# Attention in two passes over the halves of the frames, with the output projection's jobs by halves

## The chip, the cores and the metric

The kernel runs on one core of a Trainium2 chip. Time is device microseconds (us), from the start of one execution to its end; several executions are timed and their median is taken. Besides, one execution is profiled, and all rows of the profile are from that one. TensorE (PE) multiplies, VectorE (DVE), ScalarE (ACT) and GpSimd (POOL) work on tiles, and SyncE (SP) issues nearly all DMA transfers, in the order of the program. Each engine carries out its own instructions in order.

## What is computed

One block of a streaming encoder over 16 meta tokens and 1024 frames (L = 1040), model width 1024, in fp32: 8 attention heads of 64 with a forget gate and causal mask, beside a pooling branch; both go through one output projection; then a SwiGLU with its own RMS norm.

```python
def _layer(h, norm1_w, w_in, b_fgate, ...):
    proj = _rmsnorm(h, norm1_w) @ w_in
    q, k, v, fg, u = jnp.split(proj, ...)
    q, k = _rmsnorm(q, q_norm_w), _rmsnorm(k, k_norm_w)      # per head
    cum_logf = jnp.cumsum(log_sigmoid(fg + b_fgate), axis=-1)
    a_out = _forgetting_attention(q, k, v, cum_logf)
    # s = q.k / 8 + cum_logf[t] - cum_logf[s], s <= t; softmax; @ v
    p_out = pooled(u) @ w_pool * pool_scale
    h = h + jnp.concatenate([a_out, p_out], -1) @ w_out
    n2 = _rmsnorm(h, norm2_w)
    return h + (silu(n2 @ w_gate) * (n2 @ w_up)) @ w_down
```

## The kernel before

A product of fp32 operands is made of three matmuls: each operand is split into a high part (ACT rounds it) and a low part (POOL or DVE subtracts), and high x high, low x high and high x low are summed in PSUM. Tiles are 128 partitions by up to 512 columns; the frames are held in two halves of 512 columns, `b` = 0 and 1.

The stages follow each other: input projections and the pooling branch (to some 247 us), attention (to some 478 us), gate and up, and the down projection. Between attention and gate/up lies the second norm, made for each half by itself.

**Attention's units.** The list `units` (L757) sets the order of pairs (head h, half b): head by head with both halves, and for the last two heads both first halves, then both second halves. A unit with b = 0 has three steps, one with b = 1 has seven; a step is one to three tiles of 128 key rows. In a step, `front` makes the scores `st` on PE (L672 to L675) and two exps on ACT, the rounded `ph` (L682) and the full `p` (L683); `mid`, one step later, subtracts them into `pl` (L689) on POOL, each fourth on DVE (`SUBV`); `back`, three steps later (`LA`), multiplies with v into `pv` (L702 to L704). After a unit's last step come Ln and Exp of the sum on ACT (L713, L714) and three passes on DVE (L720 to L723) that divide. With every second head, a background piece splits the result into `mh` and `ml` (L731, L732).

Ahead of a unit its row maxima must be known. `mx_steps` makes scores `s` on PE (L620 to L623) and reduces them on DVE (L624); `mt` collects them into `Mc` (L636 to L638), PE transposes it (L643), and ACT writes it into the operand Q (L644). The table `MAXN` says how many of these pieces run in each step of each unit, for the unit after it.

**Operands.** `stack(h)` (L573 to L586) loads Q1, Q2, K1 and K2 of a head for both halves, six large transfers over 64 partitions each and two small ones; `vload(h)` loads v. The split operands lie in DRAM from the projections on.

**Jobs that fill PE.** The output projection is cut into jobs that `fill` takes from the queue `fill_q`, as many a step as the table `FILL` says. `out_job` (L543) makes a half of one of eight row tiles: first 16 half-jobs for the pooling branch (12 matmuls `o`, L496 to L498), then 16 for head pairs 0 and 1 (6 matmuls). DVE adds each to h (L555). The w_out operand of a job is loaded two jobs ahead and split one job ahead (L525 ACT, L526 POOL). Head pairs 2 and 3 have jobs of their own, `c_job` (L831), with operands `wc` that `wc_prep` splits once (L826, L827); they also square the result (L836, ACT) and sum the squares for the second norm (L840). The eight `c_job`s of half 0 and then `first_half` stand at the queue's end.

**The passage.** `first_half` (L922) sends half 0 to DRAM, and puts pieces into the work queue `pq`: the second norm (`norm2`: split, two matmuls with ones `n` L859 and L860, then L861, Ln and Exp L865 and L866, three passes L146 to L148), the eight normalised tiles (`x_half` L875, `x_split` L880 and L881, tile `cb`), and between them `w0_prep`, the splits of gate/up's first weights. `work` takes `XW` pieces a step in the last unit. After attention `first_pair(0, second_half)` runs gate and up's first two products on half 0 (matmuls `gu`, L1277 to L1279), 12 for each of eight tiles `cb`, and between them `second_half` runs the `c_job`s of half 1 (table `CJ`), after which the norm of half 1 follows.

Of the kernel before, what the change touches and what calls it, by code (L numbers as in the profile page):

```python
# [48 lines left out]
def block_kernel(ctx, tc, hT, n1w, w_f, w_v, w_u, w_qk, b_f, qnw, knw, w_pool, pscale, w_out, n2w, w_g, w_up, w_d, outT):  # L49
# [453 lines left out]
    jobs = []

    def out_load(x):
        mix_of, ks, m, first = jobs[x]
        n = 128 * sum(k1 - k0 for k0, k1 in ks)
        s, o = (hs if n <= 512 else aux)(n, FT, "wos"), 0
        for k0, k1 in ks:
            nc.sync.dma_start(s[:, o:o + 128 * (k1 - k0)], w_out[m, :, k0:k1, :].rearrange("p k f -> p (k f)"))  # L510
            o += 128 * (k1 - k0)
        return s

    def h_load(x):
        if x < len(jobs) and jobs[x][3] and h2[jobs[x][2]] is None:
            h2[jobs[x][2]] = ut(SEQ, FT, "h2")
            nc.sync.dma_start(h2[jobs[x][2]], hT[:, jobs[x][2], META:])
# [952 lines left out]
```

## Time and profile before

| | us |
|---|---|
| median of 3 runs | 1154.95 (1151.79 to 1155.16) |
| the profiled execution | 1152.21 |
| its span, first to last instruction | 1150.4 |
| PE busy in the span | 1120.1 (97%) |
| DVE, ACT, POOL busy | 779.7, 482.9, 217.2 |

The profiled execution's rows add up to its own time, 1152.21 us, and not to the median. PE's busy time is modelled from the starts of matmuls, so two rows of a timeline overlap; what a matmul costs in a stream is the distance of the starts. An idle time in brackets is that of the engine right before the row, with what ended it. The granted clock is given in parts of full speed; the two levels are 1.2 and 2.4 GHz.

### The profile page before, as it was taken

How to read it: one execution, taken by the hardware profiler on the slowest of the kernel's cores; microseconds unless marked ns; L12 is line 12 of the kernel's file. 1: busy time of each engine (PE TensorE's matmuls, PEld its weight loads, DVE VectorE, ACT ScalarE, POOL GpSimd, SP SyncE). 2: the span in 40 equal slices, each digit the busy share in tenths (PEclk: the TensorE clock that was granted, in tenths of full speed). 3: DMA queues.
4: the chain of work that ended last, by engine and by line, in shares of the span. 5: the costliest groups of instructions: out<-in, count | busy, mean ns of one | idle time of the engine just before them, and what ended most of it. 6: DMA issues, size and time to landing. Idle time of an engine off the chain costs nothing.

```text
span 1150.4 us, 14630 instructions
## 1 busy us (share of the span) xinstructions
PE 1120.1 (97%) x5327; PEld 929.0 (81%) x5327; DVE 779.7 (68%) x1292; ACT 482.9 (42%) x871; POOL 217.2 (19%) x185
## 2 busy tenths in 40 slices
PE   7999999999999999698999999999999999999998
PEld 6778899778888888486788888888888888888886
DVE  7555873774557665858876656666666679778986
ACT  7344531635556456535433232323232335344541
POOL 0011245133445366100012111211121010000000
PEclk9999999999999999899999999999999999999999
DMA  7134341664543722140213122313131389643452
GB/s 241 71 129 153 113 147 45 185 203 102 145 95 84 160 69 81 67 146 19 101 57 109 63 94 63 110 56 101 65 110 55 126 285 349 199 149 101 156 192 110
DMA packets 62424, 141.09 MB, mean 123 GB/s; under 512 B 7616, under 2 KB 18496, under 8 KB 62352
## 3 DMA queue, kind: packets, MB, share of 16 engines
q1 hardware_dynamic: 52528, 123.86, 34.1%
q10 hardware_dynamic: 9824, 16.30, 3.9%
q8 instruction: 42, 0.69, 0.2%
q14 instruction: 30, 0.25, 0.1%
HBM read 105.17 MB, written 34.77 MB: 122 GB/s over the span
## 4 chain that ended last, share of the span: by engine, by line
PE 89%; DVE 8%; ACT 2%; issue 1%; DMA 0%; ACTq 0%; SPq 0%; DVEq 0%
PE gu L1119 11%; PE gu L1120 11%; PE gu L1118 11%; PE d L1379 6%; PE d L1377 6%; PE d L1378 6%; PE pj L448 3%; PE pj L449 3%; PE pj L447 3%; PE o L496 3%; PE o L498 3%; PE o L497 3%; PE st L675 2%; DVE cb L881 2%; PE v L255 2%; PE v L257 2%
## 5 line engine op out<-in xcount | busy, mean ns | idle before, releaser
L1118 PE MATMUL gu<-cb,ws 128*128 128x512 f32 x560 | 220.5, 394 | 1.1 <-ACT ws L1108 1.1
L1119 PE MATMUL gu<-cb,ws 128*128 128x512 f32 x560 | 220.6, 394 | 0.2 <-DVE ws L1109 0.2
L1120 PE MATMUL gu<-cb,ws 128*128 128x512 f32 x560 | 220.4, 393 | 0.0
L1108 ACT ACTIVATE ws<-wst 128x512 fp32r<-128x512 f32 x120 | 70.1, 623 | 143.3 <-DVE wst L1103 97.1
L1118 PEld LDWEIGHTS gu<-cb,ws 128*128 128x128 f32 x560 | 105.2, 188 | 26.0 <-ACT ws L1108 1.5
L1119 PEld LDWEIGHTS gu<-cb,ws 128*128 128x128 f32 x560 | 105.2, 188 | 25.0 <-DVE ws L1109 0.5
L1120 PEld LDWEIGHTS gu<-cb,ws 128*128 128x128 f32 x560 | 105.2, 188 | 24.4
L1109 DVE TENSOR_TENSOR ws<-wst,ws 128x512 fp32r<-128x512 f32 x120 | 82.4, 688 | 59.6 <-ACT ws L1108 59.6
L1377 PE MATMUL d<-hd,wd 128*128 128x512 f32 x308 | 121.0, 393 | 0.0
L1379 PE MATMUL d<-hd,wd 128*128 128x512 f32 x308 | 121.0, 393 | 0.0
L1378 PE MATMUL d<-hd,wd 128*128 128x512 f32 x308 | 120.9, 392 | 0.0
L1132 POOL TENSOR_TENSOR e<-e,e 128x512 f32<-128x512 f32 x20 | 29.1, 1456 | 371.6 <-DVE e L1145 199.9
L689 POOL TENSOR_TENSOR pl<-p,ph 128x512 fp32r<-128x512 f32 (+4 forms) x66 | 72.7, 1113 | 57.7 <-ACT p L683 51.5
L448 PE MATMUL pj<-xh,wl 128*128 128x346 f32 (+2 forms) x216 | 72.8, 337 | 0.0
L449 PE MATMUL pj<-xl,wh 128*128 128x346 f32 (+2 forms) x216 | 72.8, 337 | 0.0
L447 PE MATMUL pj<-xh,wh 128*128 128x346 f32 (+2 forms) x216 | 72.8, 337 | 0.0
L624 DVE TENSOR_REDUCE mp<-s 128x1 f32<-128x264 f32 (+8 forms) x112 | 52.5, 504 | 27.8 <-PE s L623 25.6
L682 ACT ACTIVATE ph<-st 128x512 fp32r<-128x512 f32 (+4 forms) x88 | 46.2, 525 | 53.9 <-PE st L675 48.9
L1378 PEld LDWEIGHTS d<-hd,wd 128*128 128x128 f32 x308 | 57.9, 188 | 13.3
L1379 PEld LDWEIGHTS d<-hd,wd 128*128 128x128 f32 x308 | 57.8, 188 | 13.3
L1377 PEld LDWEIGHTS d<-hd,wd 128*128 128x128 f32 x308 | 57.8, 188 | 13.2
L1048 ACT ACTIVATE hd<-wst 128x512 fp32r<-128x512 f32 x77 | 48.0, 623 | 36.3 <-issue 27.1
(288 smaller groups left out, 2385.4 us busy)
## 6 DMA issues: line engine op xcount, KB each, us to landing
wst<-in_w_d SPq DMA_DIRECT2D x77, 256.0 KB, 6.1
wst<-in_w_g SPq DMA_DIRECT2D x22, 512.0 KB
wst<-in_w_up SPq DMA_DIRECT2D x22, 512.0 KB, 3.4
wst<-hidd SPq DMA_DIRECT2D x22, 512.0 KB, 3.4
K<-kd SPq DMA_DIRECT2D x24, 260.0 KB, 7.5
vsd<-vst SPq DMA_DIRECT2D x16, 384.0 KB, 2.3
Q<-qd SPq DMA_DIRECT2D x24, 256.0 KB, 6.0
wst<-in_w_d SPq DMA_DIRECT2D x11, 512.0 KB, 3.6
```

The costliest lines, as they stand in the source:

```text
L447: mm(p[:, :n], wh[:, W], xh[k][:, o:o + n], start=k == 0, stop=False)
L448: mm(p[:, :n], wl[:, W], xh[k][:, o:o + n], start=False, stop=False)
L449: mm(p[:, :n], wh[:, W], xl[k][:, o:o + n], start=False, stop=k == KT - 1)
L689: sub.tensor_tensor(pl[:sz, o0:o1], p32[:sz, o0:o1], f(ph)[:sz, o0:o1], op=OP.subtract)
L1108: A.activation(t[:, :512], src, AF.Copy)
L1109: E.tensor_tensor(t[:, 512:], src, f(t)[:, :512], op=OP.subtract)
L1118: mm(p, w[:, W], c[:, :512], start=k == 0, stop=False)
L1119: mm(p, w[:, Wl], c[:, :512], start=False, stop=False)
L1120: mm(p, w[:, W], c[:, 512:], start=False, stop=k == 3)
L1377: mm(p, w[:, W], h[:, LO], start=i == 0, stop=False)
L1378: mm(p, w[:, Wl], h[:, LO], start=False, stop=False)
L1379: mm(p, w[:, W], h[:, HI], start=False, stop=i == NPR - 1)
```

## The change

- `units` becomes all heads' first halves, then all heads' second halves (`n` counts them, 0 to 15).
- `stack(h, b)` and `vload(h, b)` load the operands of one unit: 512 columns of Q, and of K and v what the half needs (640 or 1040 rows of K). K and Q are loaded three to four units ahead, v one unit ahead.
- Jobs are made for a half: 16 for the pooling branch, 8 for half 0 over all four head pairs (12 matmuls, with the norm's squares), 8 for half 1 over pairs 0 and 1, and 8 for half 1 over pairs 2 and 3, which run between gate/up's matmuls. These last ones too load and split their operand one by one; `wc_prep` is gone.
- `first_half` is inserted at place 24 of the queue of jobs. The weight splits `w0_prep` go to the work queue at the start of the last unit, ahead of whatever `first_half` brings. `XW` is 2, and from unit 12 on each step takes one piece.
- `MAXN`, `FILL` and the first call of `max_next` are set for the new order.

```diff
-MAXN = [(2, 0, 0), (0, 2, 2, 2, 2, 2, 2)] * 6 + [(2, 2, 2), (2, 2, 2), (0, 1, 1, 1, 1, 0, 0), (0,) * 7]
+MAXN = [(2, 2, 1)] * 7 + [(3, 3, 3)] + [(2, 2, 1, 1, 1, 1, 1)] * 8
 SUBV = 4
 MID = 1
 VST = 3
 AGE = 2
 RAMP = 1
-FILL = [11 / 37] * 8 + [.75] * 6 + [2] * 2
-CJ, XW = {1: (0, 1), 2: (2, 3), 3: (4, 5), 4: (6, 7)}, 3
+FILL = [8 / 24] * 8 + [12 / 35] * 5 + [4 / 14] * 2 + [2 / 7]
+CJ, XW, XN = {1: (0, 1), 2: (2, 3), 3: (4, 5), 4: (6, 7)}, 2, 12
...
-    def out_job(x, b, p=None):
-        mix_of, ks, m, first = jobs[x]
-        if b == 0:
-            if x not in wo:
-                wo[x] = out_split(out_load(x))
+    def out_job(x, b):
+        mix_of, k0, k1, m, halves, norm = jobs[x]
+        if b == halves[0]:
             for y in (x + 1, x + 2):
                 if y < len(jobs) and y not in wo:
                     wo[y] = out_load(y)
             h_load(x)
             h_load(x + 1)
-        p = out_mm(mix_of(), wo[x], b) if p is None else p
+        p = out_mm(mix_of(b), wo[x])
         S = slice(512 * b, 512 * b + 512)
-        post.append(lambda: V.tensor_tensor(h2[m][:, S], p, h2[m][:, S], op=OP.add))
-        if b == 1:
+
+        def add():
+            V.tensor_tensor(h2[m][:, S], p, h2[m][:, S], op=OP.add)
+            if norm:
+                sq = hs(512, FT, "sq2")
+                A.activation(sq, h2[m][:, S], AF.Square)
+                if m == 0:
+                    acc[b] = sq
+                else:
+                    (V if b else G).tensor_tensor(acc[b], acc[b], sq, op=OP.add)
+        post.append(add)
+        if b == halves[0] and x + 1 < len(jobs):
+            wo[x + 1] = out_split(wo[x + 1])
+        if b == halves[-1]:
             wo.pop(x)
-        elif x + 1 < len(jobs):
-            wo[x + 1] = out_split(wo[x + 1])
-
-    def out_fill(need, mix_of, ks, ms, first):
-        for m in ms:
+
+    def out_jobs(need, mix_of, k0, k1, halves, norm=False):
+        for m in range(KT):
             x = len(jobs)
-            jobs.append((mix_of, ks, m, first))
-            fill_q.extend([(need, lambda x=x: out_job(x, 0)), (need, lambda x=x: out_job(x, 1))])
-
-
-
-    vhb = []
+            jobs.append((mix_of, k0, k1, m, halves, norm))
+            if need is not None:
+                fill_q.extend((need, lambda x=x, b=b: out_job(x, b)) for b in halves)
...
-    def stack(h):
+    def stack(h, b):
+
 
         dma = nc.sync.dma_start
         T, B = slice(0, 64), slice(64, 128)
         R = (T, B)[h % 2]
-        Q1, Q2, K1, K2 = heads[h] = ut(SEQ, FR, "Q1"), ut(SEQ, FR, "Q2"), ut(L, FR, "K1"), ut(L, FR, "K2")
-        q, k = [[qkd[c][h // 2, a, R, :n] for a in range(2)] for c, n in (("q", SEQ), ("k", L))]
+        n = 640 + 400 * b
+        Q, K1, K2 = ut(1024, FR, "Q"), ut(n, FR, "K1"), ut(n, FR, "K2")
+        Q1, Q2 = Q[:, :512], Q[:, 512:]
+        heads[h, b] = Q1, Q2, K1, K2
+        q, k = [[qkd[c][h // 2, a, R, S] for a in range(2)] for c, S in (("q", slice(512 * b, 512 * b + 512)), ("k", slice(0, n)))]
         for t, P, src in ((Q1, T, q[0]), (K1, T, k[0]), (Q1, B, q[0]), (K1, B, k[1]), (Q2, T, q[1]), (K2, T, k[0])):
             dma(f(t)[P], src)
-        dma(f(Q2)[64:66], f(KAT[0])[4 * h + 2:4 * h + 4, :SEQ])
-        dma(f(K2)[64:68], f(KAT[0])[4 * h:4 * h + 4])
...
-    units = [(h, b) for h in range(NH - 2) for b in range(2)] + [(h, b) for b in range(2) for h in (NH - 2, NH - 1)]
-    out_fill(0, lambda: mixp, ((4, 8),), range(0, 8), True)
-    out_fill(4, lambda: mixa[0:2], ((0, 2),), range(0, 8), False)
+    units = [(h, b) for b in range(2) for h in range(NH)]
+    out_jobs(0, mix_pool, 4, 8, (0, 1))
+    out_jobs(4, mix_heads(0, 4), 0, 4, (0,), True)
+    out_jobs(6, mix_heads(0, 2), 0, 2, (1,))
+    out_jobs(None, mix_heads(2, 4), 2, 4, (1,), True)
+    C1 = len(jobs) - KT
...
-    for m in range(KT):
-        fill_q.append((7, lambda m=m: c_job(m, 0)))
-
     def first_half():
         spill(range(KT), 0)
         norm_pieces(0, NB[0])
-        xp, wp = x_pieces(0), [[(None, lambda u=u, n=n: w0_prep(u, n)) for n in ns for u in range(2)] for ns in ((11, 21), (12, 22))]
-        pq.extend(xp[:5] + wp[0] + xp[5:] + wp[1])
-
-    fill_q.append((7, first_half))
+        pq.extend(x_pieces(0))
+
+    fill_q.insert(24, (4, first_half))
...
-        max_next(2)
+        max_next(3)
...
-        if b == 0 and 0 < h < NH - 2:
-            stack(h + 1)
-        if (h, b) == (NH - 3, 1):
-            stack(NH - 1)
-        if (h, b) == (NH - 2, 0):
-            bg.extend([lambda i=i: wc_prep(i) for i in range(4)])
-        if b == 1 and h < NH - 2 or (h, b) == (NH - 1, 0):
-            background(99)
-            vload(h + 1 if b else h)
+        while len(heads) < min(len(units), n + (4 if n < 6 else 3)):
+            stack(*units[len(heads)])
+        if n == len(units) - 1:
+            pq.extend((None, lambda u=u, c=c: w0_prep(u, c)) for c in (11, 21, 12, 22) for u in range(2))
+            w0_load()
...
-            if n == len(units) - 1:
+            if n == len(units) - 1 and x:
                 work(XW)
-                if x == 4:
-                    w0_load()
+            elif n >= XN:
+                work(1)
...
+            if x == 2 and n + 1 < len(units):
+                vload(*units[n + 1])
...
-            c_job(m, 1)
-            spill((m,), 1)
-        if k == max(CJ):
+            flush()
+            out_job(C1 + m, 1)
+            if m:
+                spill((m - 1,), 1)
+        if k == max(CJ) + 1:
+            flush()
+            spill((KT - 1,), 1)
```

Line numbers shift by some ten to twenty; the same work stands at L629 to L633 (`s`), L652 (transposes), L681 to L684 (`st`), L711 to L713 (`pv`), L501 to L503 (`o`), L847 and L848 (`n`), L1259 to L1261 (`gu`).

Order of PE at the start of attention, second unit's transposes; before:

```order
L620 MATMUL s_2435<-K_334_2011,Q_332_2009 128x348
L623 MATMUL s_2435<-K_335_2012,Q_333_2010 128x348
L620 MATMUL s_2439<-K_334_2011,Q_332_2009 128x346
L623 MATMUL s_2439<-K_335_2012,Q_333_2010 128x346
L620 MATMUL s_2443<-K_334_2011,Q_332_2009 128x346
L622 MATMUL s_2443<-maskB,ident 128x128
L623 MATMUL s_2443<-K_335_2012,Q_333_2010 128x346
L643 MATMUL mt_2452<-ident,Mc_830 68x128 x4
L672 MATMUL st_2463<-Q_332_2009,K_334_2011 128x512
```

and after:

```order
L681 MATMUL st_2427<-Q_2009,K_333_2010 128x400
L683 MATMUL st_2427<-maskA,ident 128x128
L684 MATMUL st_2427<-Q_2009,K_334_2011 128x400
L629 MATMUL s_2439<-K_382_2239,Q_2238 128x144
L631 MATMUL s_2439<-maskB,ident 128x128
L632 MATMUL s_2439<-K_383_2240,Q_2238 128x144
L629 MATMUL s_2444<-K_382_2239,Q_2238 128x272
L631 MATMUL s_2444<-maskB,ident 128x128
L632 MATMUL s_2444<-K_383_2240,Q_2238 128x272
L652 MATMUL mt_2449<-ident,Mc_830 68x128 x4
L681 MATMUL st_2455<-Q_2009,K_333_2010 128x272
```

Before, the transposes follow directly on the last score of the maximum that they need; after, scores of two maxima for a third unit stand between.

Order of PE where the second norm's two sums (`n`) stand, before:

```order
L703 MATMUL pv_4854<-ph_4742,vh_2458 64x512
L704 MATMUL pv_4854<-pl_4782,vh_2458 128x512
L672 MATMUL st_4858<-Q_803_4036,K_805_4038 128x512
L674 MATMUL st_4858<-maskA,ident 128x112
L675 MATMUL st_4858<-Q_804_4037,K_806_4039 128x512
L859 MATMUL n_1006_4868<-wh_4847,ones 128x512
L860 MATMUL n_1006_4868<-wl_4848,ones 128x512
L702 MATMUL pv_4854<-ph_4777,vh_2458 128x512
L703 MATMUL pv_4854<-ph_4777,vh_2458 64x512
```

and after:

```order
L501 MATMUL o_5049<-mh_3936,wo_5031 128x512
L502 MATMUL o_5049<-mh_3936,wo_5031 128x512
L503 MATMUL o_5049<-mh_3936,wo_5031 128x512
L847 MATMUL n_1050_5059<-wh_5015,ones 128x512
L848 MATMUL n_1050_5059<-wl_5016,ones 128x512
L1259 MATMUL gu_5074<-cb_5084,w_999_4851 128x512
L1260 MATMUL gu_5074<-cb_5084,w_999_4851 128x512
```

The sums stood between the scores of the last unit's fifth step and a `pv`, with 36 matmuls behind them to the first `gu`; now they stand behind the last job and right ahead of the first `gu`.

Order of DVE at the same norm, before (L861 is its first pass, L146 to L148 the last ones, L875 the normalised tiles, L720 to L723 the division of the last unit but one):

```order
L689 TENSOR_TENSOR pl_4816<-p_983_4776,ph_4777 128x512
L133 TENSOR_TENSOR wl_4848<-sq_962_4678,wh_4847 128x512
L720 TENSOR_TENSOR pv_4629<-pv_4629,r_4827 64x512
L721 SCALAR_TENSOR_TENSOR r_4827<-pv_4629,r_4827 64x512
L723 SCALAR_TENSOR_TENSOR a_930_4561<-pv_4629,r_4827 64x512
L861 TENSOR_SCALAR t_1007_4869<-n_1006_4868 128x512
L146 TENSOR_TENSOR tm_1017_4897<-t_1007_4869,r_1008_4873 128x512
L147 SCALAR_TENSOR_TENSOR tm_1017_4897<-tm_1017_4897,r_1008_4873 128x512
L148 SCALAR_TENSOR_TENSOR r_1008_4873<-tm_1017_4897,r_1008_4873 128x512
L875 SCALAR_TENSOR_TENSOR h_329_1992<-h_329_1992,n_100,r_1008_4873 128x512
L875 SCALAR_TENSOR_TENSOR h_331_2007<-h_331_2007,n_100,r_1008_4873 128x512
L689 TENSOR_TENSOR pl_4924<-p_1014_4888,ph_4889 128x400
```

and after (the same passes are L849, L146 to L148 and L863; L729 to L732 the division of the last unit, L739 its split, L551 the last job's add):

```order
L551 TENSOR_TENSOR h_510_2848<-o_5024,h_510_2848 128x512
L849 TENSOR_SCALAR t_1051_5060<-n_1050_5059 128x512
L729 TENSOR_TENSOR pv_4933<-pv_4933,r_5043 64x512
L730 SCALAR_TENSOR_TENSOR r_5043<-pv_4933,r_5043 64x512
L732 SCALAR_TENSOR_TENSOR a_1022_4929<-pv_4933,r_5043 64x512
L739 TENSOR_TENSOR mh_5070<-a_1022_4929,mh_5070 128x512
L551 TENSOR_TENSOR h_567_3099<-o_5049,h_567_3099 128x512
L146 TENSOR_TENSOR tm_1058_5078<-t_1051_5060,r_1052_5064 128x512
L147 SCALAR_TENSOR_TENSOR tm_1058_5078<-tm_1058_5078,r_1052_5064 128x512
L148 SCALAR_TENSOR_TENSOR r_1052_5064<-tm_1058_5078,r_1052_5064 128x512
L863 SCALAR_TENSOR_TENSOR h_329_1992<-h_329_1992,n_100,r_1052_5064 128x512
L863 SCALAR_TENSOR_TENSOR h_331_2007<-h_331_2007,n_100,r_1052_5064 128x512
```

The division of the last unit, its split and an add now stand between the norm's first pass and its last ones.

## Rows read from the trace of the kernel before

**Rows 1.** The page: busy time of each engine, and the granted TensorE clock in 40 slices.

```profile
PE 1120.1 (97%) x5327; PEld 929.0 (81%) x5327; DVE 779.7 (68%) x1292; ACT 482.9 (42%) x871; POOL 217.2 (19%) x185
...
PEclk9999999999999999899999999999999999999999
```

**Rows 2.** The page: the chain that ended last, shares of the span.

```profile
PE 89%; DVE 8%; ACT 2%; issue 1%; DMA 0%; ACTq 0%; SPq 0%; DVEq 0%
```

**Rows 3.** PE's waits, 200 to 600 us: us in total, times, longest.

```profile
PE pv L704 <- DVE pl L689: 6.4, 2, 3.4
PE mt L643 <- DVE Mc L638: 2.2, 2, 1.5
PE n L859 <- ACT wh L130: 2.0, 1, 2.0
...
PE o L496 <- ACT mh L731: 0.8, 1, 0.8
PE n L860 <- DVE wl L133: 0.7, 1, 0.7
```

**Rows 4.** Timeline of PE: start, duration, count, and in brackets the idle time before.

```profile
257.89 0.43 PE L643 MATMUL mt<-ident,Mc 128*68 128x128 f32 x4 [1.54 <-DVE Mc L638]
...
259.00 0.50 PE L675 MATMUL st<-Q,K 68*128 68x512 f32 x1 [0.39 <-ACT Q L644]
```

**Rows 5.** Timeline of PE where attention ends and gate/up begins.

```profile
471.71 0.48 PE L704 MATMUL pv<-pl,vh 128*128 128x400 f32 x1 [3.08 <-DVE pl L689]
...
476.01 0.59 PE L704 MATMUL pv<-pl,vh 128*128 128x272 f32 x1 [3.36 <-DVE pl L689]
...
477.62 0.80 PE L1277 MATMUL gu<-cb,w 128*128 128x512 f32 x1
...
482.05 0.49 PE L1278 MATMUL gu<-cb,w 128*128 128x512 f32 x1
482.37 0.40 PE L1279 MATMUL gu<-cb,w 128*128 128x512 f32 x1
...
485.18 0.40 PE L1279 MATMUL gu<-cb,w 128*128 128x512 f32 x1
```

**Rows 6.** Timeline of DVE and ACT: the first half's second norm.

```profile
465.55 0.67 DVE L861 TENSOR_SCALAR t<-n 128x512 f32<-128x512 f32 x1
...
466.92 0.63 ACT L866 ACTIVATE r<-r 128x512 f32<-128x512 f32 x1
...
467.58 0.69 DVE L146 TENSOR_TENSOR tm<-t,r 128x512 f32<-128x512 f32 x1 [1.36 <-ACT r L866]
...
470.55 0.63 ACT L880 ACTIVATE cb<-h 128x512 fp32r<-128x512 f32 x1 [2.21 <-DVE h L875]
```

**Rows 7.** Groups by line and shape, 250 to 478 us: busy us, mean ns of one.

```profile
L555 DVE TENSOR_TENSOR h<-o,h 128x512 f32<-128x512 f32 x26 | 17.9, 687 | 24.9 <-PE o L498 24.8
...
L525 ACT ACTIVATE wo<-wos 128x256 fp32r<-128x256 f32 x8 | 3.3, 414 | 0.1
...
L526 POOL TENSOR_TENSOR wo<-wos,wo 128x256 fp32r<-128x256 f32 x8 | 5.9, 738 | 8.0 <-ACT wo L525 8.0
...
L689 POOL TENSOR_TENSOR pl<-p,ph 128x512 fp32r<-128x512 f32 x36 | 46.4, 1296 | 30.0 <-ACT p L683 23.7 <-PE pv L704 3.6 <-issue 1.7
L682 ACT ACTIVATE ph<-st 128x512 fp32r<-128x512 f32 x48 | 28.5, 595 | 28.5 <-PE st L675 24.3 <-POOL pl L689 3.7
...
L836 ACT ACTIVATE sq<-h 128x512 f32<-128x512 f32 x8 | 5.1, 632 | 6.9 <-DVE h L834 6.9
```

**Rows 8.** Busy time by stretch, last columns granted clock, DMA share, GB/s; and the page's loads.

```profile
385.00:390.00 5.00, 5.00 (x36) 4.51 (x35) 1.44 (x3) 3.31 (x7) 2.15 (x3) 1.00 1.04 218
445.00:450.00 5.00, 5.00 (x25) 3.96 (x25) 1.39 (x3) 3.03 (x8) 3.07 (x3) 1.00 0.36 139
475.00:480.00 5.00, 3.99 (x13) 3.35 (x14) 5.00 (x10) 2.63 (x6) 0.00 (x0) 0.50 0.02 5
...
K<-kd SPq DMA_DIRECT2D x24, 260.0 KB, 7.5
```

More of the change, by code (lines that the diff above doesn't have):

```diff
@@ L486, in block_kernel, with mix_pool, mix_heads, out_mm @@
     h2 = [None] * KT
-    mixa = []
-    def out_mm(mix, w, half):
+    mixa = {}
+    def mix_pool(b):
+        return [[t[:, 512 * b:512 * b + 512] for t in x] for x in mixp]
+    def mix_heads(p0, p1):
+        return lambda b: [(mixa[i, b][:, :512], mixa[i, b][:, 512:]) for i in range(p0, p1)]
+    def out_mm(mix, w):
         p = ps("o")
-        S = slice(512 * half, 512 * half + 512)
         n = len(mix)
@@ L495, in out_mm @@
             W = slice(128 * k, 128 * k + 128)
-            mm(p, w[0][:, W], h[:, S], start=k == n - 1, stop=False)
-            mm(p, w[1][:, W], h[:, S], start=False, stop=False)
-            mm(p, w[0][:, W], l[:, S], start=False, stop=k == 0)
-        return p
-    fill_q = []
-    split_done = []
-    jobs = []
+            mm(p, w[0][:, W], h, start=k == n - 1, stop=False)
+            mm(p, w[1][:, W], h, start=False, stop=False)
+            mm(p, w[0][:, W], l, start=False, stop=k == 0)
+        return p
+    fill_q, split_done, jobs, wo = [], [], [], {}
+    acc, post = [None, None], []
     def out_load(x):
-        mix_of, ks, m, first = jobs[x]
[L507 to L511, printed above, removed]
-        return s
[L514 to L517, printed above, removed]
+        _, k0, k1, m = jobs[x][:4]
+        s = hs(128 * (k1 - k0), FT, "wos")
+        nc.sync.dma_start(s, w_out[m, :, k0:k1, :].rearrange("p k f -> p (k f)"))
+        return s
     def out_split(s):
         n = s.shape[1]
-        if n > 512:
-            return split_w(s, n, aux, A, G)
         t = aux(2 * n, FR, "wo")
@@ L527, in out_split, with h_load @@
         return h, l
-    wo = {}
-    post = []
+    def h_load(x):
+        if x < KT and h2[x] is None:
+            h2[x] = ut(SEQ, FT, "h2")
+            nc.sync.dma_start(h2[x], hT[:, x, META:])
     def flush():
@@ L797, in block_kernel @@
             h_load(1)
-            stack(0)
-            vload(0)
+            stack(*units[0])
+            vload(*units[0])
+            stack(*units[1])
         if 2 <= k < 6:
@@ L812, in block_kernel @@
         if x == 2:
-            stack(1)
+            stack(*units[2])
     s0.pop(0)()
@@ L817, in block_kernel @@
     fin()
-    acc = [None, None]
-    wc = []
-    def wc_prep(i):
-        s = hs(512, FT, "wos")
-        nc.sync.dma_start(s.rearrange("p (m c) -> p m c", m=2), w_out[2 * i:2 * i + 2, :, 2:4, :].rearrange("m p k f -> p m (k f)"))
-        t = ut(1024, FR, "wc")
-        A.activation(t[:, :512], s, AF.Copy)
-        G.tensor_tensor(t[:, 512:], s, f(t)[:, :512], op=OP.subtract)
-        for m in range(2):
-            wc.append((t[:, 256 * m:256 * m + 256], t[:, 512 + 256 * m:768 + 256 * m]))
-    def c_job(m, b):
-        p = out_mm(mixa[2:4], wc[m], b)
-        S = slice(512 * b, 512 * b + 512)
-        V.tensor_tensor(h2[m][:, S], p, h2[m][:, S], op=OP.add)
-        sq = hs(512, FT, "sq2")
-        A.activation(sq, h2[m][:, S], AF.Square)
-        if m == 0:
-            acc[b] = sq
-        else:
-            (V if b else G).tensor_tensor(acc[b], acc[b], sq, op=OP.add)
     def spill(ms, b):
```

44 lines of the change are left out of this document (22 added, 22 removed).

## The prediction

> **What bounds the kernel now.** The page first: PE is busy for 97% of the span at the full granted clock in all slices but one [rows 1], and the chain that ended last is 89% PE, 8% DVE, 2% ACT, with no DMA [rows 2]. So the end is set by PE's work. The change leaves that work as it is (5257 PE rows before and after), and what can be won or lost is only where PE stands idle or runs at the lower clock. The waits of PE between 200 and 600 us say where that is today [rows 3]: a row maximum that comes late (mt on Mc, 2.2 us), and above all the passage from attention to gate/up: two waits of pv for the probabilities' low part (6.4), the norm's sums (2.0 and 0.7) and one output job (0.8). The timeline of PE shows the places: 1.54 and 0.39 us in the second unit of attention [rows 4], which leaves 0.7 of mt's 2.2 for one later place; then 3.08 and 3.36 us at 468 to 476 us, and after them ten gu matmuls between 477.62 and 482.05 us at 0.44 us each, where the twelve from 482.37 to 485.18 go by 0.23 [rows 5]. That is the lower of the clock's two levels: 475 to 480 us has 0.50 granted [rows 8], behind idle stretches.
>
> In sum the passage costs before: idle 3.08 + 3.36 + 2.0 + 0.7 + 0.8 = 9.9 us [rows 3, 5]; ten slow gu matmuls 4.43 - 10 x 0.23 = 2.1, and some 0.8 for nine short slow ones ahead of them; and about 1.5, since a matmul behind a wait begins 0.1 to 0.4 later than its wait ends. Together 14.3 us.
>
> **The change, part by part.**
>
> *The second unit's maximum.* Before, the second unit is (0,1), with nine reduces, and its mt stands right behind the last s matmul. After, it is (1,0) with five, and behind its last s stand an st and two maxima of a third unit. The wait goes: -(1.54 + 0.39) and 0.4 of restart = **-2.3**. Both ends: -2.3, or -1.0 if ACT's copy still comes late.
>
> *Small waits inside.* The other 0.7 of mt and its restart belong to the old meeting of units: **-0.9**. In its place new ones must be expected. A first-pass unit has 16,576 columns on PE (st 3200, s 3200, pv 4032, one job of 6144), at 0.23 us for 512 that is 7.45, and with what the short matmuls cost over their columns about 8.15 us (an estimate). ACT has some 5.7 us in it (six exps 3.3, the end's Ln and Exp 1.2, Q's bias rows 0.6, splits 0.6) and DVE 6.3 (five reduces 2.1, the maximum's end 0.7, the unit's end 2.1, an add 0.7, a subtraction 0.7), so either can be late at a meeting point without being the bound. In the second pass a unit has 18 us on PE up to the 13th and 14.5 in the next two, against ACT's 13.4 and 11.3. From below 0, from above about one wait of 0.7 for every third unit, 3.5; I take **+1.5**, since before shows two or three in fifteen units.
>
> *Loads per unit.* A pass-1 unit loads 885 kB of Q and K (six transfers), 492 kB of V and about 393 kB of w_out and h. At the 218 GB/s that 385 to 390 us shows with the engines' share at 1.04 [rows 8], all of it would take 8.1 us; if only Q and K go at that rate and the rest as 445 to 450 us suggests (139 GB/s at a share of 0.36, so up to 386), 6.4 us. Both are below 8.15, and stacks are issued three units ahead, where a K load needs 7.5 us to land [rows 8]. So the cover is PE's own 8.15 us, and I take **0**; what it costs if the cover is gone is the slower rival. SP's issues (eight for a stack at some 0.6 us, one V load, one w_out, half an h) take 6 to 7 us of the same unit.
>
> *The end of attention.* This is the part that decides. `first_half` (spills, second norm, normalised pieces) is put at place 24 of the queue of fill jobs, but six jobs have been taken by then, so it stands behind all the half-0 jobs and six of the half-1 jobs, and runs in the last unit; ahead of it in the work queue are the eight first splits of gate/up's weights. The order of PE shows the result: the norm's two sums stand behind the last pv and the last job, and the first gu follows directly. Three terms:
>
> (a) The last unit. PE has 17,472 columns of st and pv and two jobs of six matmuls: 7.85 + 2.76 = 10.6 us, 1.5 for each of seven steps. ACT has two exps a step (1.19, in all 8.3), eight weight splits at 0.63, two job splits at 0.41 and the end's Ln and Exp, 1.2: 15.4 us [rows 6, 7], so it falls behind by 4.8. A step's scores are used three steps later, and of these 4.5 us the exps and POOL's 1.30 use 2.8, so 1.7 are slack: 3.1 idle, and about 1 for POOL, where a job's split of 0.74 stands ahead of a subtraction. **4.1 us** (0 to 6).
>
> (b) The norm in the open. From the end of the sums: t 0.67 [rows 6], behind it on DVE the last unit's three steps of about 0.7, ACT's mh 0.63, DVE's ml 0.69, the last job's add 0.69 [rows 7], Newton's three steps of 0.69, the first normalised piece 0.75, ACT's cb 0.63 [rows 6]: 0.67 + 2.1 + 0.63 + 0.69 + 0.69 + 2.07 + 0.75 + 0.63 = **8.2 us** in which PE has nothing (in before the same chain ran from 465.55 to 471.2 beside other work).
>
> (c) The lower clock behind it: as before, 2.1 + 0.8 = **2.9** (1.4 to 2.9).
>
> 15.2 against 14.3: **+0.9**; the job that waited 0.8 for mh is free after, which the 14.3 holds already.
>
> *Second-half jobs by halves.* The wc tiles were split once ahead; now each of the last eight jobs has its load, ACT's 0.41 and POOL's 0.74 [rows 7] between gu's groups. Most are covered by 12 gu matmuls (2.8 us). The split for the sixth stands on ACT behind a Square that waits for an add behind two pieces on DVE (0.75 + 0.69 each), and comes about 1.3 late: **+1.3** (0 to 2.7). The second norm begins two pieces later, of which the wait for weights at 567 us gives most back: **+0.4**.
>
> Sum: -2.3 - 0.9 + 1.5 + 0 + 0.9 + 1.3 + 0.4 = **+0.9**. On the profiled run's 1152.2 us that is 1153.1; the median of the runs, 1154.95, lies 2.7 higher, which would give 1155.9. I put the forecast between: **1154.5 us**, no change that can be told (0.3%, 3.5 us, is about what a measurement here can tell).
>
> **The rivals.**
>
> *Faster, by a lighter tail.* The 4.1 us of (a) don't come, since ACT and POOL enter the last unit ahead, and neither do the 1.5 and 1.3 of small waits: -7 us, **1147.5**. For it: 0 is the lower end of each. Against: in the last unit ACT is busier than PE by these rows.
>
> *Faster, by a covered norm.* Were `first_half` run at the end of the half-0 jobs, (b) and most of (c) would lie under four units of attention: -11, **1143.5**. It is what the place 24 reads like. Against it is the order, where the sums stand last.
>
> *Slower, by the loads of pass 1.* K and Q come as 128 and 160 KB instead of 256 and 260. If the smaller ones move a tenth more slowly than the 218 of [rows 8], 195 GB/s, a unit needs 9.1 us of loads against 8.15, and seven units lose 6.6: **1161**. It decides from the point where the whole moves below 217 GB/s. For it: engines at a share of 1.04 there already. Against: V, w_out and h don't go at that rate. The Trainium skill's page "SBUF — State Buffer" (The DMA setup-cost knee) speaks for it: transfers should be as large as possible over 128 partitions, since each has a fixed cost of about 2 us that small ones don't make up for; its points are 224 GB/s at 256 KiB and 138 at 64 KiB, by which I estimate 190 at 160 KiB, 9.3 us for a unit and 1162.5. The trace agrees with the page at the larger size (218 with loads of 256 and 260 KB); no row has the smaller. The same page (Door 1) gives 64-partition transfers about half the ports and 196 GB/s, and 328 with 128 partitions: by these a unit loads in 7.2 us, and this rival falls.
>
> *Slower, by ACT in order in pass 2.* The half-0 jobs now carry the norm's Squares into attention. Before, ACT stood 6.9 us in front of eight of them, waiting for the add [rows 7], 0.86 each, and here the exps of the next step queue behind. With the 0.63 of the Square that is 1.5 us eight times, against 4.6 us to spare in a unit that has two or three of them. It decides if the wait for the add is as long as a step of PE, 2.6 us, for then a step's subtraction comes late; at half of the eight that would be 4 x 1.1: **1159**.
>
> **How the numbers follow.** Forecast 0.37; lighter tail 0.23; covered norm 0.07; loads 0.18; ACT in order 0.15. The first gives mostly no change; some of it, and of the others, crosses over. Faster 0.31, same 0.37, slower 0.32. The range reaches from between the two faster cases to the loads': 1145 to 1162; the forecast's own is 1151 to 1158.
>
> **What would show it.** In the profile after: no mt wait of 1.5 us in the second unit; one wait of gu for cb of some 8 us behind the norm's sums, with a granted clock near 0.5 behind it; before that, pv waiting for pl in the last unit; pass 1 with PE busy and K and Q landing before use. If that gu wait is under 4 us, (b) is wrong; if PE waits for K or Q in pass 1, the cover of the loads was wrong; if PE waits for pl in the units with Squares, ACT's rival is right.

## The result, and the profile after

The median of four runs is **1163.15 us** (1161.48 to 1164.40) against 1153.63 for the kernel before on the same chip (1151.79 to 1155.16): a ratio of 1.0082, 95% interval 1.0060 to 1.0105. The change makes the kernel slower by some 9.5 us. The forecast was 1154.5, no change; the range ended at 1162.

The profiled execution took 1163.44 us, its span is 1161.5 (before 1152.21 and 1150.4). The page of after, the parts that answer to [rows 1, 2]:

```profile
PE 1124.5 (97%) x5327; PEld 931.4 (80%) x5327; DVE 786.6 (68%) x1286; ACT 486.6 (42%) x883; POOL 231.8 (20%) x195
...
PEclk9899999989999999799999999999999999999999
...
PE 86%; DVE 6%; issue 3%; ACT 2%; POOL 1%; DMA 1%; SPq 0%; ACTq 0%; POOLq 0%; DVEq 0%
```

PE has as many rows as before and 4.4 us more busy time. Of the clock's slices (29 us each) three stand lower than in [rows 1]: the second, in the projections, which the change doesn't touch, the one from 232 to 261 us and the one from 465 to 494 us; PE's share of the chain falls from 89% to 86%. So the loss is idle time and low clock, above all at the start and at the end of attention. PE's waits of after, 200 to 640 us (total, times, longest), which answer to [rows 3]:

```profile
PE gu L1259 <- ACT cb L868: 10.9, 2, 8.5
PE pv L713 <- POOL pl L698: 5.2, 4, 1.6
PE gu L1261 <- DVE cb L869: 2.4, 1, 2.4
PE mt L652 <- DVE mp L617: 1.9, 1, 1.9
PE o L501 <- ACT wo L520: 0.9, 1, 0.9
...
PE o L501 <- ACT mh L738: 0.8, 1, 0.8
...
PE s L632 <- DMA K<-kat: 0.7, 1, 0.7
```

The wait of `gu` for the first tile `cb` (8.5 us; the rest of the 10.9 is the other half's norm, at 539 us) and three of the four waits for `pl` (1.64, 1.46 and 1.40; the fourth is 0.71 at 422 us) lie in the passage, as the prediction had it. The wait of `mt`, which the prediction removed, is there still. The trace puts it down to `mp`, a fill of a buffer that DVE makes at 254.83 us; what the transposes read is `Mc`, which DVE ends at 254.88.

To place the loss I took the start of the first transposes `mt` as a mark (247.44 us before, 246.33 after; up to there the programs do the same work), and counted, from there, by how much PE lies behind its columns at 0.23 us for 512. The columns are added up over the matmuls, 1,879,936 of them from the mark in both kernels. From the mark to the end after is 12.2 us longer than before. The spans differ by 1.1 less, because the stretch ahead of the mark happened to be shorter.

| stretch | after minus before, us | predicted |
|---|---|---|
| first unit (to 20,000 columns from the mark) | +3.1 | -2.3 |
| rest of attention (to 360,000, 439 us in after) | +2.6 | +0.6 |
| passage, with the jobs of the second half (to 500,000, 526 us) | +5.6 | +2.2 |
| from there to the end | +0.9 | +0.4 |
| sum | +12.2 | +0.9 |

A boundary inside attention is good to 1 us at best: the units come in another order, and short matmuls cost more than their columns (those of 16 columns start 0.10 us apart at 466.09 us in after), so the difference is 8.3 us at 150,000 columns and 5.1 at 300,000 with no wait of over 0.8 us in either kernel between. The same 12.2 us can be split by kind. From the mark PE stands idle for 24.0 us in after and 16.8 before (waits of over 0.25 us), which is 7.2 of it. The granted clock is at its lower level for 23.9 us in after and for 13.7 before, up to 600 us; half of such a stretch, without the idle time in it, is lost, which makes 9.4 and 5.1 us, another 4.3. So a third of the loss is not waiting but slow matmuls.

**The start of attention.** Timelines of after: PE (first three rows), then DVE (three) and POOL (one) at the same place; start, duration, and in brackets the idle time ahead.

```profile
255.03 0.61 PE L652 MATMUL mt<-ident,Mc 128*68 128x128 f32 x4 [1.89 <-DVE mp L617]
...
258.37 0.63 PE L501 MATMUL o<-mph,wo 128*128 128x512 f32 x1
258.80 0.63 PE L502 MATMUL o<-mph,wo 128*128 128x512 f32 x1
```

```profile
252.69 0.17 DVE L645 TENSOR_REDUCE mx<-mp 128x4 f32<-128x12 f32 x1
252.88 1.02 DVE L646 TENSOR_SCALAR Mc<-mx 128x4 fp32r<-128x4 f32 x1
253.94 0.94 DVE L647 SCALAR_TENSOR_TENSOR Mc<-mx,Mc 128x4 fp32r<-128x4 f32 x1
```

```profile
252.60 2.25 POOL L698 TENSOR_TENSOR pl<-p,ph 128x512 fp32r<-128x512 f32 x2 [2.25 <-ACT p L692]
```

The reduce over the maxima is done at 252.86, in time. The two passes behind it work on four numbers a partition, and take 1.02 and 0.94 us, while the same pair takes 0.17 each where POOL is idle beside it (273.90 and 274.11). They end at 253.90 and 254.88, and POOL's two subtractions beside them end at 253.87 and 254.85. Behind PE's wait the matmuls stand 0.43 us apart for 512 columns instead of 0.23. Granted clock there (the last columns are clock, DMA share and GB/s), first after and then before:

```profile
254.00:256.00 2.00, 0.97 (x7) 1.01 (x8) 1.55 (x4) 0.33 (x1) 0.85 (x1) 0.74 0.33 77
256.00:258.00 2.00, 2.00 (x11) 2.00 (x10) 0.00 (x0) 0.67 (x2) 0.00 (x0) 0.50 0.75 226
258.00:260.00 2.00, 2.00 (x7) 1.69 (x6) 1.09 (x2) 0.54 (x2) 0.00 (x0) 0.50 1.03 258
260.00:262.00 2.00, 2.00 (x6) 1.52 (x5) 0.00 (x0) 0.00 (x0) 0.00 (x0) 0.55 0.98 211
```

```profile
256.00:258.00 2.00, 0.46 (x5) 0.22 (x3) 1.90 (x7) 0.00 (x0) 0.00 (x0) 1.00 0.00 0
258.00:260.00 2.00, 1.61 (x9) 1.11 (x10) 0.36 (x1) 1.04 (x2) 0.00 (x0) 1.00 0.00 0
```

So 1.89 us of idle time were followed by nearly seven at the lower level (255.03 to 261.8), and before's 1.54 and 0.39 [rows 4] by none.

**The passage.** Timeline of PE in after, answering to [rows 5]:

```profile
468.50 0.50 PE L713 MATMUL pv<-pl,vh 128*128 128x512 f32 x1 [1.46 <-POOL pl L698]
...
470.87 0.80 PE L713 MATMUL pv<-pl,vh 128*128 128x512 f32 x1 [1.40 <-POOL pl L698]
...
478.63 0.40 PE L848 MATMUL n<-wl,ones 128*128 128x512 f32 x1
487.49 0.79 PE L1259 MATMUL gu<-cb,w 128*128 128x512 f32 x1 [8.46 <-ACT cb L868]
488.08 0.63 PE L1260 MATMUL gu<-cb,w 128*128 128x512 f32 x1
...
490.21 0.52 PE L1259 MATMUL gu<-cb,w 128*128 128x512 f32 x1
```

From 470.87 to 476.90 and again from 487.49 to 490.57 the matmuls stand at the lower level's distance. Between lies the norm in the open: DVE runs its passes almost end to end from 479.07 (the norm's first) to 486.8, with one gap of 0.70 us, and the first piece goes from DVE through ACT to PE:

```profile
479.07 0.69 DVE L849 TENSOR_SCALAR t<-n 128x512 f32<-128x512 f32 x1 [3.11 <-PE n L848]
479.79 0.71 DVE L729 TENSOR_TENSOR pv<-pv,r 64x512 f32<-64x512 f32 x1
...
483.25 0.69 DVE L551 TENSOR_TENSOR h<-o,h 128x512 f32<-128x512 f32 x1
483.85 0.68 DVE L146 TENSOR_TENSOR tm<-t,r 128x512 f32<-128x512 f32 x1
...
486.02 1.41 DVE L863 SCALAR_TENSOR_TENSOR h<-h,n,r 128x512 f32<-128x512 f32 x2
```

### The profile page after: what moved, and what is told of

The parts are those of the page before. It is cut to its first block, busy times and chain, and to the rows that moved or that the text cites. A ratio compares the mean times of both kernels' runs of the same rounds, so it can differ in the third digit from the quotient of the medians.

```text
span 1161.5 us, 14772 instructions
## 1 busy us (share of the span) xinstructions
PE 1124.5 (97%) x5327; PEld 931.4 (80%) x5327; DVE 786.6 (68%) x1286; ACT 486.6 (42%) x883; POOL 231.8 (20%) x195
## 4 chain that ended last, share of the span: by engine, by line
PE 86%; DVE 6%; issue 3%; ACT 2%; POOL 1%; DMA 1%; SPq 0%; ACTq 0%; POOLq 0%; DVEq 0%
PE gu L1104 10%; PE gu L1103 10%; PE gu L1102 10%; PE d L1365 6%; PE d L1363 6%; PE d L1364 6%; PE pj L448 3%; PE pj L447 3%; PE pj L449 3%; PE o L501 2%; PE o L502 2%; PE o L503 2%; PE st L684 2%; PE v L255 2%; PE s L632 2%
## 5 line engine op out<-in xcount | busy, mean ns | idle before, releaser
L698 POOL TENSOR_TENSOR pl<-p,ph 128x512 fp32r<-128x512 f32 (+3 forms) x64 | 73.6, 1162 | 40.3 <-ACT p L692 25.3
L633 DVE TENSOR_REDUCE mp<-s 128x1 f32<-128x264 f32 (+8 forms) x112 | 53.0, 505 | 33.3 <-PE s L632 30.7
L691 ACT ACTIVATE ph<-st 128x512 fp32r<-128x512 f32 (+3 forms) x88 | 46.3, 526 | 58.2 <-PE st L684 54.8
```

Source lines behind the costliest of these rows:

```text
L698: sub.tensor_tensor(pl[:sz, o0:o1], p32[:sz, o0:o1], f(ph)[:sz, o0:o1], op=OP.subtract)
```

## The experiments

All eight kernels start from the changed one, and none leaves work out. Each ratio is to runs of the kernel before that were taken with it (medians 1153.63 for after, 1152.04 for e1 to e4, 1153.16 for e5 to e8). The last three columns are of the profiled execution, in us: the time from the first transposes to the end of the span, PE's idle time in it, and what is lost at the lower level of the clock, counted as above. What is left without these two is between 880 and 883 us in all ten kernels.

| kernel | median | ratio to before, 95% | from the mark | PE idle | lost to the clock |
|---|---|---|---|---|---|
| before | 1153.63 | | 902.96 | 16.8 | 5.1 |
| after | 1163.15 | 1.0082 [1.0060, 1.0105] | 915.17 | 24.0 | 9.4 |
| e1_norm_early | 1163.58 | 1.0106 [1.0084, 1.0127] | 914.31 | 20.3 | 12.0 |
| e2_dve_subs | 1159.73 | 1.0071 [1.0051, 1.0090] | 911.72 | 22.3 | 8.1 |
| e3_both | 1159.24 | 1.0069 [1.0049, 1.0089] | 910.28 | 18.1 | 10.3 |
| e4_wc_once | 1166.08 | 1.0127 [1.0112, 1.0142] | 917.18 | 24.5 | 12.5 |
| e5_pieces_late | 1152.14 | 0.9996 [0.9985, 1.0006] | 904.96 | 16.3 | 5.8 |
| e6_loads_earlier | 1154.82 | 1.0008 [0.9998, 1.0018] | 905.53 | 16.6 | 6.1 |
| e7_piece_on_dve | 1150.37 | 0.9980 [0.9969, 0.9992] | 900.25 | 13.9 | 4.0 |
| e8_loads_alone | 1165.37 | 1.0111 [1.0089, 1.0132] | 917.19 | 24.1 | 11.7 |

**The norm brought forward (e1_norm_early).** `first_half` is put six places earlier in the queue of jobs, directly behind the last half-0 job.

```diff
-    fill_q.insert(24, (4, first_half))
+    fill_q.insert(18, (4, first_half))
```

> Only the place of first_half in the queue of jobs changes, 18 instead of 24, so that the norm of half 0 stands behind the last half-0 job, in the middle of the second pass. Theory A (the place is what laid the norm's chain open): the wait of gu for cb, 8.46 us at 487 us in the changed kernel, goes, and so does the stretch of low clock behind it (1.4 us); ahead of it the three waits of pv for POOL's pl (4.5 us in sum) may stay. Time 1153 us, 1150 to 1156. Rival B (the passage is bound by what DVE and ACT must do there, wherever the norm is emitted): the 8.5 us come back as waits of pv for pl or of gu for cb in the last two units, less than 3 us gained, 1160 to 1163 us.

Measured: 1163.58 us, ratio 1.0106; no gain, where 10 us had been expected. The wait of 8.5 us is gone, but there are others. PE's waits and the busy time by stretch (PE, PEld, DVE, ACT, POOL; then clock, DMA share, GB/s):

```profile
PE pv L713 <- POOL pl L698: 7.4, 4, 3.4
PE o L501 <- DVE h L551: 3.2, 2, 2.1
```

```profile
440.00:450.00 10.00, 9.87 (x53) 8.00 (x52) 9.82 (x17) 6.87 (x16) 6.30 (x6) 1.00 0.20 64
450.00:460.00 10.00, 7.82 (x36) 5.86 (x35) 9.87 (x18) 4.69 (x9) 3.38 (x3) 0.83 0.70 238
460.00:470.00 10.00, 6.56 (x26) 4.87 (x26) 4.58 (x7) 6.20 (x15) 6.07 (x7) 0.75 0.08 29
```

DVE is full from 440 to 460 us (in after 7.00 and 2.41 of the two stretches), and PE waits for its adds and then for late `pl`. What fills it are the eight normalised tiles, which come with the norm: a pass and a split of 0.7 us each and tile. So hiding the norm moved much of PE's idle time into attention, with 0.83 and 0.75 of clock behind it: 3.7 us less idle time than in after, and 2.6 more lost to the clock. Moving the norm, tiles and all, gains none of the 9.5 us.

**The first unit's subtractions on DVE (e2_dve_subs).** In unit 0 POOL has no subtraction, so that nothing of POOL's runs beside the two short passes.

```diff
-                mids.pop(0)(V if step % SUBV == 0 else G)
+                mids.pop(0)(V if step % SUBV == 0 or n == 0 else G)
```

> Only the subtractions pl of the first unit go to DVE instead of POOL. In the changed kernel the two last passes of the second unit's maximum (128x4, L646 and L647) took 1.02 and 0.94 us where others take 0.17, while POOL's first subtraction ran beside them; PE waited 1.89 us and ran at half clock for 6.7 us behind that. Theory C (DVE is held while POOL works): both passes take 0.17 us, the wait of mt falls from 1.89 to 0.4 us or less, the clock stays full, and 4 to 5 us are gained: 1158.5 us, 1157 to 1160. Rival D (the two passes are slow for another reason, say the transposed tile's former reader): both stay near 1 us and the time stays at 1163, or rises by the subtractions on DVE.

Measured: 1159.73 us (1157.64 to 1161.15, after 1161.48 to 1164.40; the intervals of the two ratios overlap). In the trace it is 3.5 us less than after from the mark, and 4.7 less at 20,000 columns (PE is 1.9 us behind its columns there, in after 6.6, before 3.5). Timeline of DVE, and then of PE:

```profile
251.33 0.17 DVE L645 TENSOR_REDUCE mx<-mp 128x4 f32<-128x12 f32 x1
251.53 0.17 DVE L646 TENSOR_SCALAR Mc<-mx 128x4 fp32r<-128x4 f32 x1
251.74 0.17 DVE L647 SCALAR_TENSOR_TENSOR Mc<-mx,Mc 128x4 fp32r<-128x4 f32 x1
```

```profile
252.05 0.41 PE L652 MATMUL mt<-ident,Mc 128*68 128x128 f32 x4 [0.27 <-DVE Mc L647]
```

The two passes take 0.17 us each, the wait falls from 1.89 to 0.27, and the granted clock is 1.00 in each stretch of 2 us from 252 to 260. POOL's subtractions had held DVE's passes, and the order of PE was as good as the prediction thought: the reduces were in time.

**Both (e3_both).**

> Both edits: first_half at place 18 and the first unit's subtractions on DVE. If the two losses are independent (theories A and C) the gains add up: 10 + 4.5 under 1163, 1148.5 us (1146 to 1152), faster than the kernel before at 1153.6. If one of them only hid a later wait (a load of pass 1, ACT in order in pass 2), less than the sum: 1153 or more.

Measured: 1159.24 us, not the 1148.5 expected. From the mark it gains 1.4 on e2, so the norm early still gives next to nothing: 3.4 and 2.1 us for `pl` and the adds stand as in e1.

**The last jobs' operands split once (e4_wc_once).** The w_out operands of the last eight jobs are loaded and split in the 14th unit, in four pieces of 512 columns, as the kernel before did.

```diff
+    def wc_prep(i):
...
+        if n == 13:
+            bg.extend([lambda i=i: wc_prep(i) for i in range(4)])
```

> Only the operands of the last eight jobs change: they are loaded in four transfers and split once in the 14th unit, as in the kernel before, and the jobs between gu's matmuls only multiply. Theory: the waits of o for its operand at 508 us (0.9 on ACT and 0.5 on POOL) and their restarts go, 1.5 to 2 us; four splits more in the 14th unit are covered. 1161.3 us (1160 to 1162.5). Rival: the splits cost the 14th unit as much as they save later, or the second half's norm waits the longer: 1163 or more.

Measured: 1166.08 us, 2.0 more than after from the mark. The waits of the jobs at 508 us (0.90 and 0.50) are gone, which gains 2.0 locally. POOL gives it back: in unit 13 (the 14th) two of the splits and another stand ahead of a subtraction.

```profile
431.90 2.53 POOL L835 TENSOR_TENSOR wc<-wos,wc 128x512 fp32r<-128x512 f32 x2 [0.85 <-DMA wos<-in_w_out]
434.38 0.74 POOL L521 TENSOR_TENSOR wo<-wos,wo 128x256 fp32r<-128x256 f32 x1
435.07 1.26 POOL L698 TENSOR_TENSOR pl<-p,ph 128x512 fp32r<-128x512 f32 x1
```

```profile
436.39 0.50 PE L713 MATMUL pv<-pl,vh 128*128 128x512 f32 x1 [1.49 <-DVE Mc L646]
```

The trace puts PE's 1.49 us down to DVE, whose pass ended at 436.37; but what `pv` reads is POOL's `pl`, ended at 436.33 behind the splits. Another 1.6 us comes from a low clock behind a K wait of 0.99 us (0.81 granted from 330 to 335 us), which in after, with 0.70 of wait, was not there (1.00). It lies 100 us ahead of the first of these splits, so it is not their doing: at 150,000 columns e4 is already 1.9 us behind after, and at the end 2.0. So the jobs' waits are a real term of some 2 us, near the prediction's 1.3 (up to 2.7), and splitting the operands together costs as much elsewhere in this trace. Why the median lies 3 us above after's isn't shown.

**The tiles left late (e5_pieces_late).** As e3, but only the norm is early; its normalised tiles come in the last unit, behind the first weight splits, one a group of matmuls.

```diff
     def first_half():
         spill(range(KT), 0)
         norm_pieces(0, NB[0])
-        pq.extend(x_pieces(0))
...
+            pq.extend(x_pieces(0))
...
-                work(XW)
+                work(XW if x < 5 else 0)
...
-        work(XW)
+        work(1)
```

> As e3_both (norm at place 18, first unit's subtractions on DVE), but the norm alone is taken early: the normalised tiles (16 DVE passes of some 0.7 us and 8 on ACT) stay behind the weight splits, one piece in each of the last three steps and the rest between gu's matmuls. Theory E (in e1 and e3 it was the tiles, not the norm, that made DVE the bound of the 13th to 15th units: 9.8 of 10 us busy at 440 to 460 us, PE waiting for DVE's add, and for pl): those waits go, gu waits under 2 us, and 7 to 9 us are gained on e3: 1151 us, 1149 to 1153, level with the kernel before or a little faster. Rival F (the passage costs some 14 us wherever its parts stand, because DVE, ACT and POOL have more to do there than PE): 1157 or more.

Measured: 1152.14 us, ratio 0.9996 [0.9985, 1.0006], no different from before. From the mark that is 5.3 us less than e3 and 6.8 less than e2. DVE by the same stretches:

```profile
440.00:450.00 10.00, 10.00 (x62) 8.59 (x60) 6.04 (x13) 6.66 (x13) 4.07 (x4) 1.00 0.66 204
450.00:460.00 10.00, 8.38 (x35) 6.42 (x35) 2.07 (x4) 6.60 (x17) 6.65 (x7) 0.83 0.31 119
```

DVE is at 6.04 and 2.07 us where e1 had 9.82 and 9.87, and `gu` waits for no tile behind attention. With e1 and e3 this shows that the norm can be hidden, and that it paid here only without its tiles. The edit also takes the work pieces behind attention one at a time instead of two; no run separates that.

**Operands one unit earlier (e6_loads_earlier, e8_loads_alone).** Each unit's Q and K are issued one unit earlier in the first pass; e6 on top of e5, e8 on the changed kernel alone.

```diff
-        while len(heads) < min(len(units), n + (4 if n < 6 else 3)):
+        while len(heads) < min(len(units), n + (5 if n < 5 else 4 if n < 6 else 3)):
```

> As e5_pieces_late, and K and Q are loaded five units ahead instead of four up to the fifth unit. In all kernels of the new order PE waits 0.7 to 1.0 us for the first K of the second pass at 319 to 326 us, whose loads stand on the queue behind a v load that waits for its tile. Theory: that wait goes, and with it the chance of a lower clock behind it: 1 to 2 us under e5. Rival (loads bound the first pass): issuing them earlier moves the wait to another unit, no gain.

Measured: 1154.82 us, 0.6 more than e5 from the mark, where a gain of 1 to 2 us had been expected. PE's one wait for K is there still (0.86 us at 321 us). In SP's timeline Q and K of the first second-pass unit are issued at 312.05 us, right behind a load of v at 311.58 for which SP had waited since some 304; so they came no earlier (their small Q load 69.0 us from the mark, in e5 68.5).

> The changed kernel with K and Q loaded one unit earlier up to the fifth unit, and nothing else. If loads were what made the change slow (the rival of the prediction with 1161 us), this gains several us; by the traces it takes away one wait of 0.7 us: 1162 us, within 1.5 us of the changed kernel.

Measured: 1165.37 us, 2.0 more than after from the mark, with the K wait 0.73 us (0.70). The 2.0 are clock: the idle time is the same within 0.1 us, and 2.3 us more are lost at the lower level. Neither kernel gains anything, and PE has only that one wait for an operand's load. Inside the first pass the operands of four units did come 8 to 11 us earlier (the small Q load at 17.5, 27.9, 36.0 and 46.4 us from the mark, in after at 28.1, 36.2, 46.4 and 55.3), and nothing was gained by it. The loads are not what costs the 9.5 us. For the first unit of the second pass a larger lead wasn't reached, since SP is held by v.

**A background split on DVE (e7_piece_on_dve).** As e6, with the low part of the sixth head's result, second half, on DVE, so that it isn't ahead of POOL's subtractions.

```diff
-                    (V if h == NH - 1 else G).tensor_tensor(t[:, 512:], ...
+                    (V if h == NH - 1 or b and h == NH - 3 else G).tensor_tensor(t[:, 512:], ...
```

> As e6_loads_earlier, and the low part of the sixth head's result in the second half (1.28 us on POOL at the last unit's start) is subtracted on DVE. Theory G (pv waits for pl at the last unit's start because POOL does this and a job's split first): the wait of 1.6 us falls under 0.5: 1 to 1.5 us under e6. Rival: POOL's split of 0.74 and DVE's hold on it are enough to keep the wait, no change.

Measured: 1150.37 us, ratio 0.9980 [0.9969, 0.9992]: faster than the changed kernel, and level with the one before or 0.2% under it, which is little beside the spread of the executions (1148.00 to 1154.22). From the mark it gains 5.3 us on e6, where 1 to 1.5 had been expected. Ahead of the last unit the wait for `pl` falls from 1.62 us (454.05) to 0.35 (452.61), and one near its end from 2.07 to 0.83. These and a smaller K wait make 2.7 us of idle time, and 2.1 more are clock; e6 and then e7:

```profile
455.00:460.00 5.00, 5.00 (x18) 3.88 (x17) 0.69 (x1) 2.73 (x6) 3.39 (x4) 0.75 0.14 45
```

```profile
455.00:460.00 5.00, 5.00 (x27) 4.19 (x26) 2.89 (x5) 4.36 (x10) 3.07 (x5) 1.00 0.09 30
```

## Why the prediction was wrong

**The step that failed first: "The second unit's maximum ... The wait goes", -2.3.** It came to +3.1, which is 5.4 of the 11.3 us between the predicted and the measured sum: the wait stayed (1.89 us), and a low clock came behind it, for which the sum had no term there. What was right is that the reduces are in time (252.86 us). What was left out is the engine beside: in the new order POOL subtracts two tiles just when DVE makes its two passes over four columns, and these last until POOL's end, 1.0 us each instead of 0.17. The prediction priced "the maximum's end" at 0.7 us as a sum of DVE's own durations, and let nothing else bear on it. The trace of before would have shown it; DVE and then POOL:

```profile
370.40 0.57 DVE L637 TENSOR_SCALAR Mc<-mx 128x4 fp32r<-128x4 f32 x1
371.01 1.21 DVE L638 SCALAR_TENSOR_TENSOR Mc<-mx,Mc 128x4 fp32r<-128x4 f32 x1
```

```profile
370.21 0.73 POOL L526 TENSOR_TENSOR wo<-wos,wo 128x256 fp32r<-128x256 f32 x1
370.91 1.28 POOL L689 TENSOR_TENSOR pl<-p,ph 128x512 fp32r<-128x512 f32 x1
```

Each of the two passes ends 0.03 us behind POOL's work beside it. From 250 to 478 us they take 261 and 298 ns in the mean before, and 518 and 423 in after. e2 removes POOL's work from that place, and comes near the predicted -2.3 (1.9 us behind the columns against 3.5 before, -1.6).

The Trainium skill's page "SBUF — State Buffer" (Who interferes with whom) has the rule: DVE and GpSimd share one pair of ports as an exclusive lock. Against a GpSimd operation that reads SBUF, a DVE operation with two inputs in SBUF, or one in a mode with two ports, needs it, and the one that comes second is blocked fully until the other has ended; reduces are never held. The trace agrees: 1.02 and 0.94 us, each ended 0.03 behind one of POOL's subtractions (253.90 and 253.87, 254.88 and 254.85), and 0.17 for the reduce that ran under the first. The first of the two passes has one input, and no row shows which mode it runs in, only that it is held.

The larger part of that miss is the clock: some 3 us lost at the lower level, behind an idle time no longer than before's two together. Neither kernel's rows say why 1.89 us lowered it and 1.54 with 0.39 didn't; that stays open.

**Small waits in attention, predicted -0.9 + 1.5 = +0.6, came to some +2.6.** PE waits in after for K (0.70), Q (0.39), `mh` (0.76), `pl` (0.71), and once 0.43 for a maximum, 3.0 us in all, near the upper end of 3.5 that the text had. Its price was taken from before, where units of a head alternate.

**The passage: right in the norm, in part by luck in (a), and its sum too small by 3.4.** The three waits for `pl` are 4.50 us where (a) said 4.1, though only two of them (2.86) are the last unit's own; the third, 1.64 at 454.86, lies at the end of the unit before, where POOL has a background split (1.29) and a job's split (1.27) ahead of its subtractions. In the last unit ACT does run without a pause, as (a) had it, but what PE waits for is POOL. ACT and then POOL:

```profile
464.35 0.59 ACT L692 ACTIVATE p<-st 128x512 f32<-128x512 f32 x1
```

```profile
466.48 0.74 POOL L521 TENSOR_TENSOR wo<-wos,wo 128x256 fp32r<-128x256 f32 x1 [3.40 <-PE st L684]
467.17 3.65 POOL L698 TENSOR_TENSOR pl<-p,ph 128x512 fp32r<-128x512 f32 x2
```

The first subtraction's input is there at 464.93, but a job's split stands ahead of it; (a) gave that about 1 us of its 4.1. The second takes 2.41 us (468.41 to 470.82), some 1.1 more than alone, beside two DVE subtractions (468.41 to 469.69). By these times it is the same hold as at the start of attention, which (a) left out as well; no run takes the two subtractions away. The norm in the open is 8.46 where (b) said 8.2, link by link; the jobs' waits are 1.40 where 1.3 stood. What was mis-sized is (c), the low clock: it comes twice, some 2.5 us from 470.87 to 476.90, behind the waits of the last unit, and 1.4 from 487.49, together 3.9 where 2.9 stood. The first stretch had no place in the sum, though (a) predicted the idle time ahead of it. And the late starts behind waits, some 1.5 us, were counted into before's 14.3 and not into after's 15.2.

**The second norm and what follows:** +0.9 against +0.4. Its two waits are 4.77 us (3.14 before), and the wait for weights, 1.08 before, is gone.

**The rivals.** *Lighter tail*: wrong, 4.5 us of waits came (POOL's two subtractions from 467.17, 3.65 us, would alone take 1.3 each [rows 7]; DVE is busy for 9.09 of the 10 us from 460). *Covered norm*, priced -11: the early place brought nothing while the tiles came with it and filled DVE (e1); with the tiles late it is worth 6.8 us from the mark (e5 against e2). *Loads of pass 1*: PE waits for one load of an operand, 0.70 us, and earlier issues gain nothing (e8). In the first pass, from 258 to 260 us and from 260 to 262, when nine tenths or more of what moves is Q and K, the DMA engines move 258 and 211 GB/s at shares of 1.03 and 0.98, where [rows 8] has 218 at 1.04. The lower rate for smaller transfers that was read from the Trainium skill's page "SBUF — State Buffer" (The DMA setup-cost knee) doesn't show there. *ACT in order*: one wait for `pl` in the second pass up to the unit before the last, 0.71 us, not four of 1.1. That the time came out near the loads' 1161 is chance.

**Chances.** The prediction saw the places of the passage and gave slower 0.32. Its range ended too low, by 1.2 us, because the terms were bounded one by one: (c) hangs on (a), and an idle time can bring a low clock with it as a second price, which no term but (c) held. Its 5257 PE rows are 5327 on both pages; that the work on PE stays the same is right.

## What to carry to other kernels

When an edit moves work in time, price a short pass on the path not by its own duration alone, but by what runs beside it on POOL at that moment. Give an idle time of PE a second price with a chance of its own, for a lower clock behind it: here it came behind some waits of 1 us and more and not behind others, and cost 1.4 to 3.4 us where it came. And a chain moved under other work has to be split: what the path needs goes early, what only hangs on it stays where its engine is free (e3 against e5).
